# An encoder block on one core: the first stage in a written order, the late expert loads in program order

## The chip, the cores and the metric

One core of a Trainium2 chip runs the whole block in one launch. The metric is the device time of one execution in microseconds (us); lower is better. Two executions differ by about 0.2% without any change.

## What is computed

The reference is one encoder layer on 512 tokens of width 1024, all in float32:

```python
u  = rmsnorm(x, g1)
cb, cc, cx, q, k, v, gc, ga = split(u @ w_in)           # 1024 1024 1024 1024 256 256 1024 1024
yc = (cb * dwconv3(cc * cx)) @ w_conv_out
q  = rope(rmsnorm(q, gq)); k = rope(rmsnorm(k, gk))     # 8 heads of q, 2 of k and v, width 128
ya = attention(q, k, v) @ w_attn_out
x1 = x + (sigmoid(gc) * yc + sigmoid(ga) * ya) @ w_o
out = x1 + moe(rmsnorm(x1, g2))   # 8 groups of 8 experts, best group, best 2 of its experts, width 512
```

## The kernel before

The kernel has two halves. The **mixer** is everything up to `x1`. Its matrices are multiplied in three products: a weight is loaded as float32 (`raw`), cast to a high part (`wh`, ScalarE, L157), and the rest is its low part (`wl`, VectorE, L158); the activations are split in the same way (`uH`, `uL`), and high by high, high by low and low by high are summed in PSUM. `stage` loads and splits one weight slice of 512 KB; `raw`, `wh` and `wl` have two buffers each.

The work is a list of units (`unit`). `run_units` goes through it and stages the weight of the next unit ahead. The framework then orders each engine's instructions by itself: an instruction may run ahead of earlier ones of the same engine when it is ready sooner by the framework's own estimate. `keep_in_program_order` pins one instruction behind what was written before it on its engine.

The units, in order:

- The **first stage**: two halves of v (`v_unit`). Row sums of squares on ScalarE (`norm_stat`), the power -1/2 on POOL, an identity scaled by it (`norm_diag`), and a matmul of x with that identity (`norm_in`, tile `tpu`) which turns and norms a tile of 128 tokens at once; then the gain, the cast and the subtraction, and `o_v`. At its end `rope_tables_in` loads the rope table and the constants.
- The two k heads (`k_unit`), and for each `k_norm_unit`: `norm_rstd` sums squares by matmul (`st_ps`), the power runs on POOL (L262), and a matmul spreads it (`bc`). One cc projection (`fill`) stands between the two.
- For each of 8 heads: q, scores, softmax, turning, values, with the projections cc, cx and cb as fillers.
- The gates gc and ga with `yc`, then `ya`, then `o` (8 slices of `w_o`; the last two are multiplied at the end, bank by bank), and the router's logits.

The **expert half** reads all 64 experts: 192 weight tiles of 2 MB each, in ten rotating slots of the memory that the mixer also uses, and one more tile. `load_weight` issues one on SP's queue. `load_unit` places nine of them into the mixer's list, as its slots come free: 0, 1 and 2 in the gate stages, 3 and 4 behind `ya` units, 5 to 8 behind the `o` units in `LOADS`. `order` gives the slots: 9, 5, 8, 0, 1, 3, 4, 2, 6, 7.

Of the kernel before, what the change touches and what calls it, by code (L numbers as in the profile page):

```python
# [19 lines left out]
P = 128  # L20
T = 512
# [18 lines left out]
def block_kernel(ctx, tc, x, norm1_g, w_in, conv_w, q_norm_g, k_norm_g, w_conv_out,  # L40
                 w_attn_out, w_o, norm2_g, w_group, w_router, w1, w3, w2, rope, out):
    nc = tc.nc
    V, A, G, TE = nc.vector, nc.scalar, nc.gpsimd, nc.tensor
# [34 lines left out]
    def load_x(t):  # L78
        nc.sync.dma_start(xt[:, t, :], x[t * P:(t + 1) * P, :])

    load_x(0)
    load_x(1)
    g1 = cst.tile([P, NK], F32, name="g1")
    A.dma_start(g1, norm1_g[0].rearrange("(k p) -> p k", p=P), allow_slow_non_contiguous=True)
# [6 lines left out]
    warm = cst.tile([P, 1], F32, name="warm")  # L91

# [6 lines left out]
    def load_constants():  # L99
        for nm, src in (("k", k_norm_g), ("q", q_norm_g)):  # L100
            g = src[0].rearrange("(i two) -> two i", two=2)
            for h in range(2):
                for j in range(2):
                    nc.sync.dma_start(gp[nm][h * 64:(h + 1) * 64, j:j + 1], g[(h + j) % 2, :, None],
                                      allow_slow_non_contiguous=True)
        nc.sync.dma_start(cw, conv_w[0].rearrange("w (k p) -> p w k", p=P), allow_slow_non_contiguous=True)
        nc.sync.dma_start(g2, norm2_g[0].rearrange("(k p) -> p k", p=P), allow_slow_non_contiguous=True)
        nc.sync.dma_start(g2j, norm2_g[0].rearrange("(p j) -> p j", j=NK))
        nc.sync.dma_start(wr[:, :, 0:NG], w_group[0].rearrange("(k p) e -> p k e", p=P))
        nc.sync.dma_start(wr[:, :, NG:], w_router[0].rearrange("(k p) e -> p k e", p=P))  # L110
        G.tensor_tensor(wr, wr, g2[:, :, None].to_broadcast([P, NK, NG + NE]), op=OP.mult)
# [16 lines left out]
    with tc.high_priority():  # L128
        make_identity(nc, eye)
        V.tensor_copy(identr, eye)  # L130
    late_x = [lambda: (load_x(2), load_x(3)), lambda: None]

    iog = cst.tile([P, NG], F32, name="iog")
    G.iota(iog, pattern=[[1, NG]], base=-NG, channel_multiplier=0, allow_small_or_imprecise_dtypes=True)
    io32 = cst.tile([P, CAP], F32, name="io32")
    G.iota(io32, pattern=[[1, CAP]], base=0, channel_multiplier=0, allow_small_or_imprecise_dtypes=True)
    iorow = wtile("iorow")[:, :P]
    G.iota(iorow, pattern=[[1, P]], base=0, channel_multiplier=-1, allow_small_or_imprecise_dtypes=True)
    tri = cst.tile([P, P], BF16, name="tri")
    V.tensor_scalar(tri, iorow, 0.0, None, op0=OP.is_gt)  # L140
    onesb = cst.tile([P, 1], BF16, name="onesb")
    V.memset(onesb, 1.0)

    def stage(src, perm=False):
        shape = [P, src.shape[1], src.shape[2]]
        raw = pools["st"].tile(shape, F32, tag="raw", name="raw", bufs=2)
        nc.sync.dma_start(raw, src)
        if late_x:
            late_x.pop()()
# [7 lines left out]
        A.copy(h, r)  # L157
        V.tensor_tensor(l, r, h.bitcast(F32), op=OP.subtract)  # L158
        return wh, wl
# [46 lines left out]
    diags = {}  # L206

    def norm_stat(t):
        c = slice(t, t + 1)
        sq = wtile("sq", "q", 1, [P, D])  # L210
        A.activation(sq, xt[:, t, :], AF.Square, accum_out=ss[:, c])
        V.tensor_scalar(var[:, c], ss[:, c], 1.0 / D, EPS, op0=OP.mult, op1=OP.add)
        G.tensor_tensor(rstd[:, c], var[:, c], nhalf[:, c], op=OP.pow)
# [23 lines left out]
    def rope_tables_in():  # L237
        nc.sync.dma_start(rk[:, 2:4, :], rope.rearrange("a p t -> p a t"))
# [30 lines left out]
    def v_unit(half):  # L269
        def f(wt):  # L270
            if half == 0:
                vacc.extend(pa("o_v") for _ in range(NT))
            for t in range(NT):
                if half == 0:
                    if t + 2 < NT:
                        norm_stat(t + 2)
                    norm_in(t)
                    if t + 2 < NT:
                        norm_diag(t + 2)
                o = vacc[t]  # L280
                c = slice(t * P, (t + 1) * P)
                for k in range(4):
                    kk = 4 * half + k
                    mh, ml = u(kk)
                    mm(o[:, :256], mh[:, c], wt[0][:, k, :], kk == 0, False)
                    mm(o[:, :256], ml[:, c], wt[0][:, k, :], False, False)
                    mm(o[:, :256], mh[:, c], wt[1][:, k, :], False, kk == NK - 1)
                if half == 1:
                    split(vH[:, t * 256:(t + 1) * 256], vL[:, t * 256:(t + 1) * 256], o[:, :256])
            if half == 0:  # L290
                rope_tables_in()
        unit(f, cols(w_in, C_V, 256, 4 * half, 4 * half + 4))
# [3 lines left out]
    def k_unit(g):  # L296
        def f(wt):
            o = pa("o_k")
            proj(o, wt, u)
            kpart[g] = rope_apply(o, rk)  # L300
        unit(f, cols(w_in, C_K + g * HD, perm=True))

    def k_norm_unit(g):
        def f():
            fk, sq = kpart.pop(g)
            r = norm_rstd(sq)
            bc = pt("bc")
            for t in range(NT):
                mm(bc[:, t * P:(t + 1) * P], r[:, 1, t:t + 1].to_broadcast([P, P]), ident, True, True)
            V.tensor_tensor(fk, fk, bc, op=OP.mult)  # L310
            split(kH[:, g * T:(g + 1) * T], kL[:, g * T:(g + 1) * T], fk)
        unit(f)
# [127 lines left out]
    for t in range(2):  # L440
        with tc.high_priority():
            norm_stat(t)
            norm_diag(t)
    v_unit(0)
    v_unit(1)
    k_unit(0)
    k_unit(1)
    k_norm_unit(0)
    fill()
# [98 lines left out]
    def o_unit(kk):  # L548
        def f(wt):
# [9 lines left out]
            elif kk == NK - 1:  # L559
                A.activation(warm, gates["ga"](NK - 1)[:, 0:1], AF.Exp)  # L560
# [56 lines left out]

    load_unit(0)
# [9 lines left out]
    for k in range(NK):  # L628
        ya_unit(k)
        if k in (1, 3):  # L630
            load_unit(3 + k // 2)
# [6 lines left out]
    run_units()  # L638
    mixer.close()
# [267 lines left out]
    pin = tc.keep_in_program_order  # L907

# [41 lines left out]
    def finish_last(X, ws, gt2, c2, y, Sl, wl):  # L950
# [16 lines left out]
        def spread(q):  # L967
# [6 lines left out]
            for h, src in enumerate((o, kept[q])):  # L974
# [6 lines left out]
                (A if h and q == 3 else nc.sync).dma_start(ov[:, 2 * h:2 * h + 2, c0:c1], d)  # L981
# [7 lines left out]
    def store_at(t, n):  # L989
        nc.sync.dma_start(out[t * P:(t + 1) * P, n * 512:(n + 1) * 512], acc_at(t, n))  # L990

    def overflow(tiles):
        n = nc.values_load(ov_tab[0:1, NE:NE + 1], min_val=0, max_val=32)
        with tc.For_i(0, n, 1) as i:
# [12 lines left out]
            for i, w in enumerate((w1, w3, w2)):  # L1007
                src = w[bass.ds(e, 1)].rearrange("o (c p) d -> p (o c) d" if i == 2 else "o (p j) f -> p (o j) f", p=P)
                nc.sync.dma_start(tiles[i], src)
# [103 lines left out]
```

## Time and profile before

| | |
|---|---|
| median of 3 runs | 1471.94 us (1470.76 to 1472.09) |
| the profiled execution | 1478.3 us, span 1476.5 us |
| busy share of the span | TensorE 83%, VectorE 32%, ScalarE 24%, POOL 6% |
| end of the mixer's matmuls | 538.7 us |
| expert weights | 195 loads, 402.7 MB; the rate in the second half is 425 GB/s |

Times in views of the trace are us from the span's start. A line such as `L157` is a line of the kernel; all matmuls have the line of a helper, L74, so they are told apart by tiles. PE is TensorE, DVE VectorE, ACT ScalarE, and SPq the queue of the engine that issues most transfers. A matmul in float32 shows as two records. PEclk is the granted share of TensorE's full clock.

### The profile page before, as it was taken

The page shows a single profiled execution, that of the slowest core. Times are in us where ns is not written, and L with a number is a line of the kernel's source. Part 1 is how long each engine was busy: PE and PEld are TensorE (multiplying, and loading weights), DVE is VectorE, ACT ScalarE, POOL GpSimd, SP SyncE. Part 2 cuts the span into 40 slices and gives each one's busy share as a digit, 9 for nine tenths or more (in the row PEclk, how much of TensorE's full clock was granted, in tenths as well). Part 3 has the DMA queues.
Part 4 walks back from the last instruction along what each step waited for, and adds up shares of the span by engine and source line. Part 5 has one row for each costly group of instructions (what it writes and reads, how often), then busy time and mean ns, then how long its engine had stood idle before and what let it go on. Part 6 is the DMA issues. An engine that isn't in the chain of part 4 may idle for free.

```text
span 1476.5 us, 33402 instructions
## 1 busy us (share of the span) xinstructions
PE 1230.3 (83%) x15172; PEld 911.5 (62%) x15172; DVE 468.9 (32%) x943; ACT 347.6 (24%) x715; POOL 88.0 (6%) x128
## 2 busy tenths in 40 slices
PE   7999999999999988897886685876867758678587
PEld 6788888888887775664654453544545545455454
DVE  4375666623225342332122120220211212212032
ACT  4344444522222232111111111111101111111111
POOL 2200000000002001000000000000000000000000
PEclk9899999999999999999998997998989889888888
DMA  7222222243554749999999999999999999999994
GB/s 218 62 72 71 72 72 71 62 138 87 156 175 128 295 163 427 423 426 425 426 425 426 427 424 427 425 426 425 426 425 427 427 424 427 425 427 425 426 394 156
DMA packets 111664, 449.71 MB, mean 305 GB/s; under 512 B 12577, under 2 KB 85281, under 8 KB 87073
## 3 DMA queue, kind: packets, MB, share of 16 engines
q1 hardware_dynamic: 110208, 447.29, 75.2%
q8 instruction: 120, 1.97, 0.5%
q10 hardware_dynamic: 1312, 0.27, 0.1%
q14 instruction: 24, 0.19, 0.0%
HBM read 445.44 MB, written 2.10 MB: 303 GB/s over the span
## 4 chain that ended last, share of the span: by engine, by line
DMA 49%; PE 47%; issue 2%; DVE 1%; ACT 1%; POOL 0%; SPq 0%; ACTq 0%; DVEq 0%; POOLq 0%
DMA w<-in_w 48%; PE o_g L74 6%; PE h L74 4%; PE o_cc L74 3%; PE o_q L74 3%; PE o_o L74 3%; PE o_cb L74 3%; PE o_cx L74 3%; PE o_yc L74 3%; PE o_ya L74 3%; PE o_c L74 3%; PE y L74 3%; PE o_x L74 2%; PE s L74 2%; PE o_pv L74 1%
## 5 line engine op out<-in xcount | busy, mean ns | idle before, releaser
L74 PE MATMUL h<-w,X 128*32 128x128 f32 x8192 | 290.2, 296 | 109.3 <-DMA w<-in_w 87.8
L74 PEld LDWEIGHTS h<-w,X 128*32 128x32 f32 x8192 | 253.4, 119 | 154.4 <-issue 62.3
L74 PE MATMUL y<-w,gt 128*32 128x256 f32 x2048 | 165.6, 455 | 87.6 <-DMA w<-in_w 61.5
L74 PEld LDWEIGHTS y<-w,gt 128*32 128x32 f32 x2048 | 85.8, 126 | 144.6 <-issue 116.4
L904 ACT COPY Y<-y 32x256 f32<-32x256 f32 x248 | 90.2, 364 | 230.3 <-PE y L74 227.9
L158 DVE TENSOR_TENSOR wl<-raw,wh 128x1024 fp32r<-128x1024 f32 x76 | 99.3, 1309 | 131.6 <-ACT wh L157 130.1
L74 PE MATMUL o_x<-xt,pR 128*32 128x256 f32 x2048 | 133.8, 380 | 6.8 <-issue 4.6
L74 PE MATMUL o_c<-Y,S 128*128 128x512 f32 (+1 forms) x256 | 123.7, 639 | 12.6 <-ACT Y L904 12.6
L157 ACT CAST wh<-raw 128x1024 fp32r<-128x1024 f32 x76 | 80.5, 1060 | 202.7 <-PE o_g L74 67.1
L886 DVE TENSOR_TENSOR sp<-h,sg 128x128 f32<-128x128 f32 x64 | 23.4, 365 | 286.6 <-ACT sg L882 286.6
L847 DVE TENSOR_TENSOR acc<-o_c,acc 128x512 f32<-128x512 f32 x112 | 77.5, 692 | 103.9 <-PE o_c L74 103.9
L74 PEld LDWEIGHTS o_x<-xt,pR 128*32 128x32 f32 x2048 | 81.3, 110 | 40.6 <-issue 8.2
L882 ACT ACTIVATE sg<-h 128x128 f32<-128x128 f32 x64 | 17.8, 278 | 373.6 <-PE h L74 373.6
L732 DVE STREAM_TRANSPOSE X<-xs 128x256 f32<-128x256 f32 x64 | 28.5, 445 | 238.2 <-PE h L74 201.5
L74 PEld LDWEIGHTS o_c<-Y,S 128*128 128x128 f32 (+1 forms) x256 | 50.5, 203 | 82.4 <-issue 50.8
L74 PE MATMUL o_g<-u,wh 128*128 128x512 f32 x256 | 80.5, 395 | 0.0
L870 POOL TENSOR_TENSOR pR<-p,rstd 128x512 f32<-128x512 f32 x15 | 15.6, 1041 | 705.9 <-PE o_x L74 642.1
L74 PEld LDWEIGHTS o_g<-u,wh 128*128 128x128 f32 x256 | 48.2, 188 | 11.2
L74 PE MATMUL o_g<-u,wl 128*128 128x512 f32 x128 | 50.5, 395 | 0.0
L74 PE MATMUL o_o<-wh,m 128*128 128x512 f32 x128 | 41.3, 402 | 1.7 <-ACT wh L157 1.7
L74 PE MATMUL o_cc<-u,wh 128*128 128x512 f32 x128 | 41.5, 406 | 0.0
L74 PE MATMUL o_q<-u,wh 128*128 128x512 f32 x128 | 41.2, 403 | 0.0
(242 smaller groups left out, 1462.0 us busy)
## 6 DMA issues: line engine op xcount, KB each, us to landing
w<-in_w SPq DMA_DIRECT2D x191, 2048.0 KB, 39.6
raw<-in_w_in SPq DMA_DIRECT2D x52, 512.0 KB, 3.8
raw<-in_w_conv_out SPq DMA_DIRECT2D x8, 512.0 KB, 4.1
raw<-in_w_attn_out SPq DMA_DIRECT2D x8, 512.0 KB, 4.2
raw<-in_w_o SPq DMA_DIRECT2D x8, 512.0 KB, 4.4
xt<-in_x SPq DMA_DIRECT2D x4, 512.0 KB, 6.9
w<-in_w SPq DMA_DIRECT2D x4, 512.0 KB, 30.4
out<-acc SPq DMA_DIRECT2D x7, 256.0 KB, 2.4
```

What stands on the lines that cost most here:

```text
L74: return TE.matmul(o, l, r, start=start, stop=stop)
L157: A.copy(h, r)
L158: V.tensor_tensor(l, r, h.bitcast(F32), op=OP.subtract)
L732: V.transpose(X.rearrange("p j s -> p (j s)"), xs.rearrange("p j i -> p (j i)"))
L847: V.tensor_tensor(acc_at(t, n), o, xt[:, t, nsl] if first else acc_at(t, n), op=OP.add)
L870: eng.tensor_tensor(pR, p0.rearrange("p t e s -> p t (e s)"), rstd2[:, :, None].to_broadcast([P, NT, P]), op=OP.mult)
L882: A.activation(sg, h[:, 0:P], AF.Silu)
L886: V.tensor_tensor(sp.rearrange("p (c i) -> p c i", c=4), h[:, P:2 * P].rearrange("p (i c) -> p c i", c=4), sg.rearrange("p (i c) -> p c i" ...
L904: A.copy(d, y[32 * q:32 * q + 32, 0:256])
```

## The change

First, the expert loads and all weight loads from the gate stage on are pinned in program order on SP; the expert loads of the late mixer move to behind `ya` 1 and 4 and `o` 0, 2, 4 and 5. The warming Exp reads a constant instead of a gate.

Second, the first stage is written anew. The gain is loaded as one row and spread over the partitions by two matmuls (`gn`). A tile is scaled by its power and by the gain in one operation (`xs`), turned by plain transposes (`tu`), and cast and subtracted straight from the PSUM bank (`uh`, `ul`), half a tile at a time. `vm` is one of the three products of one half for one token tile. A few matmuls on the identity (`wm`) stand at the start. `V_ORDER` gives the order of all these steps, each pinned on its engine; digits are the token tile, the half, and the product.

Third, the loads of x and of the first weights have an order of their own, and the rope table and constants are loaded, pinned, at the first k unit.

Fourth, `k_norm_unit` is cut in two: both statistics (`k_stat_unit`) come ahead of the cc projection, both spreads behind it.

```diff
-LOADS = (0, 1, 2, 4)
+LOADS = (0, 2, 4, 5)
...
+V_ORDER = (
+    "wm3 gn0 gn1 wm2 ld0 lx1 lx2 lx3 ld1 sq0 rs0 xs00 wh0 xs01 tu00 uh00 wl0 tu01 sq1 vm000 ul00 vm001 "
+    "uh01 rs1 vm002 sq2 ul01 xs10 sq3 xs11 tu10 rs2 tu11 uh10 rs3 xs20 uh11 vm100 ul10 tu20 wh1 vm101 ul11 "
+    "vm102 uh20 wl1 vm010 vm200 vm110 ul20 vm201 xs21 vm011 xs30 vm202 tu21 xs31 tu30 uh21 tu31 uh30 ul21 "
+    "vm012 uh31 ul30 vm300 vs0 vm111 ul31 vm301 vm112 vm302 vs1 vm210 vm310 vm211 vm311 vm212 vm312 vs2 "
+    "vs3 "
+)
...
+                i = call(*args, **kwargs)
+                return tc.keep_in_program_order(i) if pinned else i
+            return issue
...
-    g1 = cst.tile([P, NK], F32, name="g1")
-    A.dma_start(g1, norm1_g[0].rearrange("(k p) -> p k", p=P), allow_slow_non_contiguous=True)
...
+    g1 = slot(3, [1, D], F32, "g1")
+    A.dma_start(g1, norm1_g[0][None, :])
...
+        i = SP.dma_start(raw, src)
+        if nraw[0] < 4 or late:
+            pin(i)
+        nraw[0] += 1
...
-    def norm_diag(t):
-        diags[t] = wtile("diag", "z", 1, [P, 4, P])[:, 0, :]
-        V.tensor_scalar(diags[t], ident, rstd[:, t:t + 1], None, op0=OP.mult)
-
-    def norm_in(t):
-        dg = diags.pop(t)
-        for b in range(2):
-            tp = pt("tpu")
-            tpv = tp.rearrange("p (k c) -> p k c", k=4)
-            for k in range(4):
-                mm(tpv[:, k, :], xt[:, t, (4 * b + k) * P:(4 * b + k + 1) * P], dg, True, True)
-            f = wtile("f")
-            fv = f.rearrange("p (k c) -> p k c", k=4)
-            V.tensor_tensor(fv, tpv, g1[:, 4 * b:4 * b + 4, None].to_broadcast([P, 4, P]), op=OP.mult)
-            h = uH[:, 4 * b:4 * b + 4, t * P:(t + 1) * P]
-            l = uL[:, 4 * b:4 * b + 4, t * P:(t + 1) * P]
-            A.copy(h, fv)
-            (G if b else V).tensor_tensor(l, fv, h.bitcast(F32), op=OP.subtract)
...
+    def gn(b):
+        o = psx("g_b")
+        mm(o, ones[0:1, 0:1].to_broadcast([1, P]), g1[:, b * T:(b + 1) * T], True, True)
+        V.tensor_copy(gb[:, b * T:(b + 1) * T], o)
...
+    def xs(t, b):
+        nsl = slice(b * T, (b + 1) * T)
+        V.scalar_tensor_tensor(xn[:, t, nsl], xt[:, t, nsl], rstd[:, t:t + 1], gb[:, nsl], op0=OP.mult, op1=OP.mult)
+
+    def tu(t, b):
+        tps[t, b] = (psx if t % 2 else pt)("tpu").rearrange("p (k c) -> p k c", k=4)
+        for k in range(4):
+            TE.transpose(tps[t, b][:, k, :], xn[:, t, (4 * b + k) * P:(4 * b + k + 1) * P], ident)
+
+    def u_at(t, b):
+        return (a[:, 4 * b:4 * b + 4, t * P:(t + 1) * P] for a in (uH, uL))
+
+    def uh(t, b):
+        h, _ = u_at(t, b)
+        A.copy(h, tps[t, b])
+
+    def ul(t, b):
+        h, l = u_at(t, b)
+        V.tensor_tensor(l, tps.pop((t, b)), h.bitcast(F32), op=OP.subtract)
+
+    def vm(t, half, part):
+        w, lo = ((0, 0), (1, 0), (0, 1))[part]
+        c = slice(t * P, (t + 1) * P)
+        for k in range(4):
+            kk = 4 * half + k
+            mm(vacc[t][:, :256], u(kk)[lo][:, c], w_v[half][w][:, k, :], kk == 0 and part == 0, kk == NK - 1 and part == 2)
...
+            if g == 0:
+                pinned.append(True)
+                rope_tables_in()
+                pinned.clear()
...
+    def k_stat_unit(g):
+        def f():
+            fk, sq = kpart.pop(g)
+            kpart[g] = fk, norm_rstd(sq)
+        unit(f)
+
     def k_norm_unit(g):
         def f():
-            fk, sq = kpart.pop(g)
-            r = norm_rstd(sq)
+            fk, r = kpart.pop(g)
             bc = pt("bc")
             for t in range(NT):
...
     k_unit(0)
     k_unit(1)
+    k_stat_unit(0)
+    k_stat_unit(1)
+    fill()
     k_norm_unit(0)
-    fill()
     k_norm_unit(1)
...
-                A.activation(warm, gates["ga"](NK - 1)[:, 0:1], AF.Exp)
+                A.activation(warm, nhalf[:, 0:1], AF.Exp)
...
-            nc.sync.dma_start(tile[:, :, c0:c1], src[:, :, c0:c1])
+            ld = SP.dma_start(tile[:, :, c0:c1], src[:, :, c0:c1])
+            if late:
+                pin(ld)
...
+    unit(lambda: late.append(True))
...
-        if k in (1, 3):
-            load_unit(3 + k // 2)
+        if k in (1, 4):
+            load_unit(3 + k // 4)
```

## Rows read from the trace of the kernel before

**Rows 1.** The page, part 2: share of DMA time in 40 equal slices.

```profile
DMA  7222222243554749999999999999999999999994
```

**Rows 2.** Stretches: length, PE busy (matmuls), PEclk, DMA share, GB/s.

```profile
510.00:520.00 10.00, 10.00 (x44) 1.00 0.00 0
538.00:542.00 4.00, 4.00 (x43) 1.00 0.95 369
...
700.00:1400.00 700.00, 512.70 (x9372) 0.88 1.01 426
```

**Rows 3.** Waits of SP's queue: total us, times, longest.

```profile
SPq L612 <- PE o_o L74: 28.8, 1, 28.8
```

**Rows 4.** The chain that ended last, in order: start us, us, what.

```profile
9.75 3.78 PE tpu L74 x16
...
23.73 1.79 PE tpu L74 x16
25.52 6.38 PE o_v L74 x52
...
43.04 0.80 PE st_ps L74 x8
...
44.10 2.00 POOL r L262
...
56.31 1.95 POOL r L262
...
66.15 5.57 PE o_cx L74 x24
...
588.99 7.06 PE o_c L74 x16
```

**Rows 5.** Stretches again, with the granted clock behind the matmul count.

```profile
46.00:48.00 2.00, 1.85 (x9) 0.50 0.72 208
...
60.00:62.00 2.00, 2.00 (x6) 0.50 0.28 84
450.00:452.00 2.00, 0.88 (x4) 1.00 0.00 0
```

**Rows 6.** Timeline of PE at two places late in the mixer.

```profile
449.28 0.40 PE L74 MATMUL o_ya<-OL,wh 128*128 128x512 f32 x1
451.12 0.50 PE L74 MATMUL o_ya<-OH,wl 128*128 128x512 f32 x1 [1.45 <-DVE wl L158]
...
500.85 0.40 PE L74 MATMUL o_o<-wl,m 128*128 128x512 f32 x1
502.95 1.66 PE L74 MATMUL o_o<-wh,m 128*128 128x512 f32 x6 [1.71 <-ACT wh L157]
```

**Rows 7.** Timeline of ACT: behind the second k, and at the router.

```profile
45.19 0.60 ACT L249 ACTIVATE sq<-o_k 128x512 f32<-128x512 f32 x1
...
542.78 0.23 ACT L753 ACTIVATE ex<-ex 128x32 f32<-128x32 f32 x1 [4.00 <-DVE ex L752]
```

**Rows 8.** Timeline of SP's queue: constants, and loads late in the mixer.

```profile
4.41 0.50 SPq L238 DMA_DIRECT2D rk<-in_rope  x1
...
18.00 0.58 SPq L110 DMA_DIRECT2D wr<-in_w_router  x1
...
432.31 0.81 SPq L612 DMA_DIRECT2D w<-in_w  x2
434.61 24.41 SPq L147 DMA_DIRECT2D raw<-in_w_attn_out  x5
...
478.60 0.80 SPq L612 DMA_DIRECT2D w<-in_w  x2
```

**Rows 9.** Tile raw from 425 to 520.

```profile
DMA to landing us min/median/max: 3.5/4.4/13.1
```

**Rows 10.** Groups of DVE up to 80 us, by form.

```profile
L418 DVE SCALAR_TENSOR_TENSOR cc<-mz,cw,cc 128x511 f32<-128x511 f32 x1 | 0.7, 743 | 0.0
```

**Rows 11.** DMA issues up to 40 us.

```profile
g2j<-in_norm_g SPq DMA_DIRECT2D x1, 4.0 KB, 2.6
```

More of the change, by code (lines that the diff above doesn't have):

```diff
@@ L42, in block_kernel, with __init__, __getattr__, issue @@
     nc = tc.nc
-    V, A, G, TE = nc.vector, nc.scalar, nc.gpsimd, nc.tensor
+    pinned = []
+    class Engine:
+        def __init__(self, engine):
+            self.engine = engine
+        def __getattr__(self, name):
+            call = getattr(self.engine, name)
+            def issue(*args, **kwargs):
+                i = call(*args, **kwargs)
+                return tc.keep_in_program_order(i) if pinned else i
+            return issue
+    V, A, G, TE, SP = (Engine(e) for e in (nc.vector, nc.scalar, nc.gpsimd, nc.tensor, nc.sync))
+    pin = tc.keep_in_program_order
     x = x[0]
@@ L127, in block_kernel, with stage @@
     eye = wtile("eye")[:, :P]
[L128 to L144, printed above, removed]
+    make_identity(nc, eye)
+    pinned.append(True)
+    V.tensor_copy(identr, eye)
+    nraw = [0]
+    late = []
+    def stage(src, perm=False, wait=False):
         shape = [P, src.shape[1], src.shape[2]]
         raw = pools["st"].tile(shape, F32, tag="raw", name="raw", bufs=2)
-        nc.sync.dma_start(raw, src)
-        if late_x:
-            late_x.pop()()
+        i = SP.dma_start(raw, src)
+        if nraw[0] < 4 or late:
+            pin(i)
+        nraw[0] += 1
         wh = pools["st"].tile(shape, F32R, tag="wh", name="wh", bufs=2)
@@ L156, in stage @@
             l = l.rearrange("p k (two i) -> p k two i", two=2)
-        A.copy(h, r)
-        V.tensor_tensor(l, r, h.bitcast(F32), op=OP.subtract)
+        parts = [lambda: A.copy(h, r), lambda: V.tensor_tensor(l, r, h.bitcast(F32), op=OP.subtract)]
+        if wait:
+            return (wh, wl), parts
+        for part in parts:
+            part()
         return wh, wl
@@ L267, in block_kernel @@
     vacc = []
[L269 to L292, printed above, removed]
+    vacc.extend(pa("o_v") for _ in range(NT))
@@ new lines, in block_kernel, with ld, wm @@
+    gb = slot(7, [P, D], F32, "gb")
+    xn = slot(8, [P, NT, D], F32, "xn")
+    w_v, w_parts = [], []
+    tps = {}
+    def ld(i):
+        pair, parts = stage(cols(w_in, C_V, 256, 4 * i, 4 * i + 4)[0], wait=True)
+        w_v.append(pair)
+        w_parts.append(parts)
+    def wm(n):
+        for _ in range(n):
+            mm(busy0[:, 0:P], ident, ident, True, True)
+    def gn(b):
+        o = psx("g_b")
+        mm(o, ones[0:1, 0:1].to_broadcast([1, P]), g1[:, b * T:(b + 1) * T], True, True)
+        V.tensor_copy(gb[:, b * T:(b + 1) * T], o)
@@ new lines, in sq, with rs @@
+    def sq(t):
+        junk = wtile("sq", "q", 1, [P, D])
+        A.activation(junk, xt[:, t, :], AF.Square, accum_out=ss[:, t:t + 1])
+    def rs(t):
+        c = slice(t, t + 1)
+        V.tensor_scalar(var[:, c], ss[:, c], 1.0 / D, EPS, op0=OP.mult, op1=OP.add)
+        G.tensor_tensor(rstd[:, c], var[:, c], nhalf[:, c], op=OP.pow)
+    def xs(t, b):
+        nsl = slice(b * T, (b + 1) * T)
+        V.scalar_tensor_tensor(xn[:, t, nsl], xt[:, t, nsl], rstd[:, t:t + 1], gb[:, nsl], op0=OP.mult, op1=OP.mult)
@@ new lines, in vm, with wh, wl, vs @@
+    def vm(t, half, part):
[4 more added lines that the diff above has]
+            mm(vacc[t][:, :256], u(kk)[lo][:, c], w_v[half][w][:, k, :], kk == 0 and part == 0, kk == NK - 1 and part == 2)
+    def wh(i):
+        w_parts[i][0]()
+    def wl(i):
+        w_parts[i][1]()
+    def vs(t):
+        split(vH[:, t * 256:(t + 1) * 256], vL[:, t * 256:(t + 1) * 256], vacc[t][:, :256])
+    busy0 = pt("busy0")
@@ L294, in block_kernel @@
+    steps = dict(ld=ld, lx=load_x, wm=wm, gn=gn, sq=sq, rs=rs, xs=xs, tu=tu, uh=uh, ul=ul, vm=vm, wh=wh, wl=wl, vs=vs)
+    for step in V_ORDER.split():
+        steps[step[:2]](*(int(c) for c in step[2:]))
+    pinned.clear()
     kpart = {}
@@ L297, in f @@
         def f(wt):
+            if g == 0:
+                pinned.append(True)
+                rope_tables_in()
+                pinned.clear()
             o = pa("o_k")
@@ L438, in fill @@
                 fn(k)
[L440 to L445, printed above, removed]
+    iog = cst.tile([P, NG], F32, name="iog")
+    G.iota(iog, pattern=[[1, NG]], base=-NG, channel_multiplier=0, allow_small_or_imprecise_dtypes=True)
+    io32 = cst.tile([P, CAP], F32, name="io32")
+    G.iota(io32, pattern=[[1, CAP]], base=0, channel_multiplier=0, allow_small_or_imprecise_dtypes=True)
+    iorow = wtile("iorow")[:, :P]
+    G.iota(iorow, pattern=[[1, P]], base=0, channel_multiplier=-1, allow_small_or_imprecise_dtypes=True)
+    tri = cst.tile([P, P], BF16, name="tri")
+    V.tensor_scalar(tri, iorow, 0.0, None, op0=OP.is_gt)
+    onesb = cst.tile([P, 1], BF16, name="onesb")
+    V.memset(onesb, 1.0)
     k_unit(0)
     k_unit(1)
+    k_stat_unit(0)
+    k_stat_unit(1)
+    fill()
     k_norm_unit(0)
-    fill()
     k_norm_unit(1)
@@ L638, in block_kernel @@
     run_units()
+    late.clear()
     mixer.close()
@@ L905, in expert @@
         return X
-    pin = tc.keep_in_program_order
     def combine_two(S, Y):
```

30 lines of the change are left out of this document (11 added, 19 removed).

## The prediction

> **What bounds the kernel now.** I read the page's slices first [rows 1]: the DMA engines have two tenths of work in the first third and nine from the sixteenth slice to the end, where they move 425 GB/s. So there are two stages with different limits, TensorE first (83% busy over the span) and DMA then. The chain of waits, grouped, says the same: 48% is DMA into the expert weights, the rest matmuls of the mixer. Then I asked where the two meet. The stretches of time [rows 2] show the transfers idle from 510 to 520, at 369 GB/s by 538 to 542, and at 426 from 554 to 1400. In the idle stretch SP stands 28.8 us in front of one expert load, waiting for the last o_o matmuls [rows 3]: the buffers into which the stream would run are still the mixer's. So nine expert tiles are there when the mixer ends, the stream starts with the mixer's end, and from there the time is bytes over 426 GB/s. A microsecond taken from TensorE ahead of about 538 moves the whole stream, and the end with it. A microsecond behind it is worth nothing.
>
> So the question is how far the mixer's end moves. The chain in order of time [rows 4] shows where TensorE is not streaming. Its first matmul starts at 9.75. It stands at 43.84 and at 56.05 for a POOL power of some 2 us each, and both times it comes back at half clock: the granted clock is 0.50, 1.2 GHz, from 46 to 48 and from 60 to 62 [rows 5]. It stands again late in the mixer, before 451.12 and before 502.95 [rows 6]. Everything between is back to back.
>
> **The change, part by part.**
>
> *The k norms.* Before, the order on TensorE is statistics of k0, wait for POOL, broadcast, cc, statistics of k1, wait, broadcast, q. Now both statistics, then the cc projection, then both broadcasts. From the end of the k projections to the end of q is 43.04 to 66.15 = 23.1 us [rows 4]. The work in it at full clock: two statistics of 0.80, two projections of 5.57 (the length of cx just behind), two broadcasts of 8 records at 1.79 / 16 us each, 0.9 apiece: 14.5 us. The 5.6 us of cc cover the powers: the first is issued within a microsecond of its statistics and takes 2.0; the second must wait for the copies and the square of k1 on ScalarE, 2.9 us after the projection (from the last k1 matmul to the end of its square at 45.79 [rows 7]), then 0.8, then 2.0 again, 5.9 us together against 7.2 us of cc and both statistics. What is late next: nothing by more than a few tenths. If both holes go, 23.1 - 14.5 = 8.6 is won; with the second statistics a little late I take 8.4. The lower bound is one hole only: the second is worth 10.1 - 6.5 = 3.6 (56.05 to 66.15, against one broadcast and one projection).
>
> *The rope table and the constants* move behind the loads of both k weights on SP, with the multiplications that use them pinned on VectorE. Their issue took 4.41 to 18.58 = 14.2 us of SP [rows 8]. The second k weight can be loaded when the second v weight has been split, at about 19; so the constants are out by 33.5, and the raw cc weight behind them lands 3.5 to 4.4 us later [rows 9], at some 37.5, with 2.3 us of split to follow: 39.8. TensorE wants it after both k projections, 30.4 + 11.1 = 41.5. Covered, at nothing, by those projections; without the cover every microsecond counts, and only 1.7 are in hand.
>
> *The first stage.* Gone: the scaled identity, the separate gain multiplication, the POOL subtractions. New: per token tile two scalar_tensor_tensor (0.74 each, by the row of the convolution [rows 10]), 8 transposes, two casts and two subtractions from PSUM (0.62 and 0.68 each, as today's of that size). The matmul work is the same: 64 records of 128 columns at 1.79 / 16 = 7.1, and 96 of o_v at 6.38 / 52 = 11.8, 18.9 us [rows 4]. The start goes by a new chain. The gain row (4 KB, 2.6 us to landing for the nearest transfer [rows 11], issued at about 0.7) is spread over the partitions by two matmuls of 512 columns: eight such matmuls (o_c) took 7.06 us [rows 4], 0.88 each, and twice that at the slow rate with which the first sixteen tpu records ran (3.78 us against 1.79 later). So 3.3 + 3.5 = 6.8; copy 0.69, variance 0.15, power 0.56, scaling 0.74, and hand-overs: first transpose at about 9.2, half a microsecond before today. VectorE then has 3.0 us a tile and serves one tile at a time; in its fixed order the second tile's scaling stands behind the split of the weight and the first tile's subtractions, so TensorE waits some 1.7 us at 12.4. Slow first transposes add 0.6. End: 9.2 + 18.9 + 1.7 + 0.6 = 30.4 against 31.90: 1.5 won. Bounds: at full rate from the start the row spread is 1.8 shorter and nothing is slow, 27.8 (4.1 won); with TensorE at half rate until 22, 34.9 (3.0 lost).
>
> *The expert loads.* The first one, issued at 20.37, goes to the gate stage; slot and data are wanted after 538, so this costs nothing. In the late mixer two loads of 2 MB went out together at 432.31 and two at 478.60 [rows 8], and the raw weights behind them landed up to 13.1 us after their issue, against 3.5 at best [rows 9]. That made the two stalls: 449.28 to 451.12 and 500.85 to 502.95, less 0.23 for the matmul itself [rows 6]: 1.6 + 1.9 = 3.5. Now never two in a row: after ya 1 and 4, after o 0, 2, 4 and 5. The price is that a raw load now stands behind an expert load on SP. The tightest is the third w_o slice: it follows the load that waits for the end of ya (477 with the first stall gone), so it lands about 2 + (2.1 + 0.5 MB) / 0.42 = 8.2 later plus its issue, at 486.4; split by 488.7, wanted at 488.2 to 488.7. I charge 0.3 and take 3.2. All nine tiles are in long before the mixer's end (the last is issued at about 498 for an end at 525), so the stream has the same bytes left.
>
> The Trainium skill (DMA: Bandwidth & Descriptors, Queues, rings and completion order) says that each DMA engine consumes the descriptors of one issuing queue in ring order; if it did not hold, the slice would land at 481 and the 0.3 would fall away. The late landings above agree with it.
>
> *Others.* The warming Exp reads a constant and can run at any time, so the Exp table may have to be loaded again before the softmax of the router; such a load took 1.28 us, and ScalarE is idle for 4.00 just ahead of that Exp [rows 7]: nothing, and 1.28 without that idle time.
>
> **Sum.** 8.4 + 1.5 + 3.2 = 13.1 us. The profiled execution took 1478.3 us with a span of 1476.5, 6.4 above the median of 1471.94; by the sum the next profiled one takes 1465.2, and with the same distance the median becomes **1458.8 us**.
>
> **Rivals.**
> 1. *The clock falls in the first stage.* TensorE now has two holes of some 1.5 and 1.7 us (before the first transpose and before the second tile's) where it had none after 9.75. For it: the waits of 2.00 and 1.95 for POOL at the k norms halved the clock [rows 4, 5]. Against it: idles of 1.45 and 1.71 us late in the mixer [rows 6] left it at 1.00 (the first [rows 5]). Then the stage ends near 34.9, 3.0 later than now: 8.4 - 3.0 + 3.2 = 8.6, **1463.3**. The Trainium skill (TensorE: Matmul & The Clock Gate, Part 1) says that the slow state is the default and that activity releases it, which is this rival; the trace agrees at the k norms and not at the two later idles.
> 2. *Half of the k part stays*, by a statistics matmul that waits for the square on ScalarE, or by the cc weight late behind the constants (1.7 us in hand): 3.6 + 1.5 + 3.2 = 8.3, **1463.6**.
> 3. *The shift does not reach the end.* If the expert stream were limited from its first byte, nothing would move: **1471.9**. Against it: no transfers from 510 to 520 [rows 2], and SP's long wait was for o_o and for no DMA [rows 3].
> 4. *Slower: the expert loads hold up the raw weights.* Six of them now stand ahead of a raw load on a pinned queue. The latest raw load took 13.1 - 3.5 = 9.6 us longer to land than the fastest; its slack is the 13.6 us from its issue to its use less 4.4 of landing and 2.3 of split, 6.9. So up to 2.7 us each, 16.2 in all: 1471.9 - 8.4 - 1.5 + 16.2 = **1478.2**. It turns slower when the six cost more than 9.9 / 6 = 1.65 us on average. Against it: before, two loads ahead of a raw load cost only 1.6.
>
> **How the numbers follow.** All three parts as summed, 1455 to 1463: 0.56, and 0.05 for more than that (the first stage at full rate, 1456.2, and a tail that keeps its clock). Rival 1: 0.16; rival 2: 0.13; rival 3: 0.05; rival 4: 0.05. The first forecast and rivals 1 and 2 all lie in 1452 to 1467, with room for two of them together or for a late cc weight; that leaves about 2 in 10 outside. About 0.2%, 2.9 us, can be told from no change: faster 0.89, same 0.06, slower 0.05.
>
> **What would show it.** The first o_k matmul at about 30.4 (right) or past 32 (rival 1). From the end of o_k to the end of q 15 us, with no POOL wait in the chain and a granted clock of 1.00 there. No stall before ya 3 and o 4. The mixer's last matmul at about 525.6 instead of 538.7, and the DMA stretches after it shifted by the same 13 us at the same 426 GB/s. The prediction is wrong if that shift is under 8 us, or if it is there and the tail takes it back.

## The result, and the profile after

| | before | after |
|---|---|---|
| median of 9 runs each, one chip | 1477.57 us (1470.52 to 1479.74) | 1463.68 us (1457.95 to 1466.49) |
| profiled execution, its span | 1478.3, 1476.5 | 1463.09, 1461.3 |
| mixer's last router matmul ends | 538.72 | 521.42 |

The ratio is 0.9913, 95% interval 0.9895 to 0.9932: 12.8 us won of 1477, between 10.0 and 15.5. Predicted were 13.1 won and 1458.8 us, inside 1452 to 1467. Both kernels' times fall into two groups with some 5 us between them (before: 1470.5 to 1472.1 and 1477.6 to 1479.7; after: 1457.95 and 1458.12, the others from 1462.8 up), so the 0.2% of the opening holds within a group only; what parts them is a finding of the experiments. One execution of the kernel before, in the second session of the experiments, took 2004.35 us and is left out of the ratios.

The predicted signs, in their order. The chain of waits of the kernel after, in order of time (start, us, what); in this trace all lines are L62, a wrapper's, so the tiles tell what is what:

```profile
3.43 3.72 PE g_b L62 x4
...
9.41 1.13 PE tpu L62 x4
...
20.77 1.31 PE tpu L62 x12
22.08 5.78 PE o_v L62 x48
27.86 11.16 PE o_k L62 x48
39.02 0.79 PE st_ps L62 x8
39.80 2.66 PE o_cc L62 x11
42.46 0.79 PE st_ps L62 x8
43.25 3.13 PE o_cc L62 x13
46.38 1.78 PE bc L62 x16
48.16 5.57 PE o_q L62 x24
53.74 5.57 PE o_cx L62 x24
...
420.05 44.63 PE o_ya L62 x192
464.68 42.19 PE o_o L62 x181
```

Against [rows 4]: the first o_k starts at 27.86 and not at 31.90 (30.4 was forecast). From the end of o_k to the end of q it is 14.72 us instead of 23.11, and no POOL stands in it. o_ya and o_o run as unbroken pieces; the breaks of [rows 6] are gone. The clock, in stretches (length; busy time and count of PE, PEld, DVE, ACT, POOL; granted clock; DMA share; GB/s), against [rows 5] and [rows 2]:

```profile
42.00:46.00 4.00, 4.00 (x23) 3.39 (x23) 1.26 (x3) 0.00 (x0) 2.71 (x3) 1.00 0.48 135
46.00:50.00 4.00, 4.00 (x27) 3.61 (x26) 2.65 (x4) 2.42 (x4) 0.00 (x0) 1.00 0.06 10
...
520.00:530.00 10.00, 8.74 (x128) 7.30 (x130) 7.46 (x47) 4.44 (x10) 1.34 (x3) 1.00 0.95 377
700.00:1400.00 700.00, 507.62 (x9217) 352.37 (x9213) 140.12 (x318) 105.23 (x292) 25.09 (x50) 0.89 1.01 425
```

The clock is full where it was half, and the stream is there from 520 on and not from 538, at 425 GB/s. SP's queue, against [rows 8], and the landing of the raw weights from 405 to 510, against [rows 9]:

```profile
434.82 0.57 SPq L62 DMA_DIRECT2D w<-in_w  x1
440.07 4.79 SPq L62 DMA_DIRECT2D raw<-in_w_attn_out  x2
...
468.26 0.43 SPq L62 DMA_DIRECT2D w<-in_w  x1
```

```profile
DMA to landing us min/median/max: 3.5/4.4/8.9
```

No two expert loads in a row, and the latest raw load takes 8.9 us and not 13.1. So each predicted step is there, and the mixer ends 17.3 us earlier, where 13.1 was forecast. The span is shorter by 15.2. Three questions follow: where do the 4.2 us more at the mixer's end come from, where do 2.1 of them go, and why does the ratio say 12.8?

### The profile page after: what moved, and what is told of

Same layout as the page of the kernel before. It is cut to its first block, busy times and chain, and to the rows that moved or that the text cites. A ratio compares the mean times of both kernels' runs of the same rounds, so it can differ in the third digit from the quotient of the medians.

```text
span 1461.3 us, 33363 instructions
## 1 busy us (share of the span) xinstructions
PE 1221.9 (84%) x15154; PEld 912.0 (62%) x15154; DVE 472.5 (32%) x945; ACT 346.4 (24%) x715; POOL 80.8 (6%) x124
## 4 chain that ended last, share of the span: by engine, by line
PE 52%; DMA 44%; issue 2%; DVE 1%; ACT 1%; POOL 0%; SPq 0%; POOLq 0%; ACTq 0%
DMA w<-in_w 44%; PE o_g L62 6%; PE h L62 5%; PE o_c L62 5%; PE y L62 4%; PE o_cc L62 3%; PE o_q L62 3%; PE o_cb L62 3%; PE o_cx L62 3%; PE o_ya L62 3%; PE o_yc L62 3%; PE o_o L62 3%; PE o_x L62 3%; PE s L62 2%; PE o_pv L62 2%
## 5 line engine op out<-in xcount | busy, mean ns | idle before, releaser
L62 PE MATMUL h<-w,X 128*32 128x128 f32 x8192 | 293.3, 299 | 117.8 <-DMA w<-in_w 95.5
L62 PEld LDWEIGHTS h<-w,X 128*32 128x32 f32 x8192 | 255.3, 120 | 163.7 <-issue 77.3
L62 PE MATMUL y<-w,gt 128*32 128x256 f32 x2048 | 159.3, 443 | 87.1 <-DMA w<-in_w 67.2
L62 PEld LDWEIGHTS y<-w,gt 128*32 128x32 f32 x2048 | 87.5, 124 | 139.0 <-issue 112.9
L62 ACT COPY Y<-y 32x256 f32<-32x256 f32 x248 | 90.2, 364 | 223.3 <-PE y L62 220.9
L62 DVE TENSOR_TENSOR wl<-raw,wh 128x1024 fp32r<-128x1024 f32 x76 | 100.7, 1325 | 131.0 <-ACT wh L62 129.6
L62 PE MATMUL o_x<-xt,pR 128*32 128x256 f32 x2048 | 136.0, 386 | 5.5 <-issue 3.1
L62 PE MATMUL o_c<-Y,S 128*128 128x512 f32 (+1 forms) x256 | 118.8, 618 | 12.6 <-ACT Y L62 12.6
L62 ACT CAST wh<-raw 128x1024 fp32r<-128x1024 f32 x76 | 80.6, 1060 | 199.7 <-PE o_g L62 67.1
L62 DVE TENSOR_TENSOR acc<-o_c,acc 128x512 f32<-128x512 f32 x124 | 85.7, 691 | 107.5 <-PE o_c L62 107.4
L62 DVE TENSOR_TENSOR sp<-h,sg 128x128 f32<-128x128 f32 x64 | 23.2, 362 | 284.6 <-ACT sg L62 284.6
L62 DVE STREAM_TRANSPOSE X<-xs 128x256 f32<-128x256 f32 x64 | 28.5, 445 | 251.3 <-PE h L62 214.0
L62 ACT ACTIVATE sg<-h 128x128 f32<-128x128 f32 x64 | 17.8, 278 | 385.8 <-PE h L62 385.8
L62 PEld LDWEIGHTS o_x<-xt,pR 128*32 128x32 f32 x2048 | 83.8, 111 | 38.5 <-issue 7.3
L62 PEld LDWEIGHTS o_c<-Y,S 128*128 128x128 f32 (+1 forms) x256 | 48.6, 195 | 78.3 <-issue 47.7
L62 PE MATMUL o_g<-u,wh 128*128 128x512 f32 x256 | 80.4, 395 | 0.0
L62 PEld LDWEIGHTS o_g<-u,wh 128*128 128x128 f32 x256 | 48.2, 188 | 11.1
L62 POOL TENSOR_TENSOR pR<-p,rstd 128x512 f32<-128x512 f32 x15 | 15.6, 1039 | 706.3 <-PE o_x L62 641.6
L62 PE MATMUL o_g<-u,wl 128*128 128x512 f32 x128 | 50.5, 395 | 0.0
L62 PE MATMUL o_o<-wh,m 128*128 128x512 f32 x128 | 40.7, 399 | 0.0
L62 PE MATMUL o_q<-u,wh 128*128 128x512 f32 x128 | 40.3, 396 | 0.0
L62 PE MATMUL o_cc<-u,wh 128*128 128x512 f32 x128 | 40.2, 395 | 0.0
```

Of the source, the lines that this page charges most:

```text
L62: i = call(*args, **kwargs)
```

## The experiments

Unless said otherwise a time is the median of all runs of that kernel, and a ratio is to the kernel before on the same chip (its medians there: 1473.18, 1476.62 and 1474.71 in the three sessions). All traces put together, in us ("k part": end of the k projections to the end of q; "combine": the 16 matmuls that add the outputs of the experts 60 and 61 to the sum, behind expert 61; they are the last of this kind, and a shorter tail for the last two experts follows):

| kernel | time, ratio [interval] | first o_k | k part | mixer's end | span less that | combine |
|---|---|---|---|---|---|---|
| before | | 31.90 | 23.11 | 538.72 | 937.8 | 11.86 |
| after | 1463.68, 0.9913 [0.9895, 0.9932] | 27.86 | 14.72 | 521.42 | 939.9 | 11.80 |
| e1 | 1471.04, 0.9974 [0.9957, 0.9992] | 27.95 | 21.66 | 528.44 | 941.5 | 11.74 |
| e2 | 1464.44, 0.9944 [0.9923, 0.9965] | 27.97 | 14.70 | 526.45 | 936.4 | 7.13 |
| e3 | 1468.0, 0.9955 [0.9938, 0.9973] | 30.95 | 14.71 | 524.49 | 935.1 | 7.13 |
| e4 | 1458.06, 0.9908 [0.9884, 0.9932] | 26.17 | 14.71 | 519.86 | 934.9 | 7.13 |
| e5 | 1464.93, 0.9910 [0.9883, 0.9937] | 27.97 | 14.72 | 521.50 | 942.4 | 14.02 |
| e6 | 1474.38, 1.0005 [0.9984, 1.0026] | 31.51 | 18.72 | 533.94 | 937.4 | 11.71 |
| e7 | 1468.65, 0.9952 [0.9933, 0.9971] | 32.07 | 14.72 | 530.67 | 933.5 | 7.13 |
| e8 | 1456.96, 0.9882 [0.9852, 0.9911] | 26.15 | 14.72 | 519.69 | 935.6 | 7.13 |
| e9 | 1462.75, 0.9918 [0.9898, 0.9938] | 27.86 | 14.71 | 521.42 | 940.6 | 7.13 |
| e10 | 1473.69, 0.9993 [0.9976, 1.0009] | 31.65 | 20.24 | 535.78 | 935.4 | 7.13 |
| e11 | 1459.34, 0.9902 [0.9877, 0.9927] | 26.19 | 14.71 | 519.72 | 937.5 | 7.13 |
| e12 | 1462.68 (one run) | 27.96 | 14.72 | 524.35 | 936.6 | 7.13 |

### The first stage: e3 and e4

e3 is the kernel after with the turns of the rows as matmuls with the identity:

```diff
-            TE.transpose(tps[t, b][:, k, :], xn[:, t, (4 * b + k) * P:(4 * b + k + 1) * P], ident)
+            mm(tps[t, b][:, k, :], xn[:, t, (4 * b + k) * P:(4 * b + k + 1) * P], ident, True, True)
```

> The changed kernel with each of the 32 plain transposes made a float32 matmul with the identity, all else in place. Theory: a transpose shows one record of 0.11 us and a matmul two, so the first stage has 32 records or 3.5 us more of TensorE work, its end goes from 27.9 to about 31, and the time up by 3 to 3.5 us, to about 1466.5. Rival, that the first stage is bound by VectorE's chain and not by TensorE: its end moves by less than 1 us.

Its chain:

```profile
15.26 2.05 PE tpu L62 x16
...
22.52 2.68 PE tpu L62 x24
25.20 5.75 PE o_v L62 x48
30.95 9.05 PE o_k L62 x39
```

24 records where the kernel after has 12. The tile has 64 records against 32, the stage ends at 30.95 against 27.86, and the mixer ends 3.07 later. A plain transpose of a float32 tile is one record, a matmul of the same shape is two, at the same 0.11 us each. And 30.95 is within 0.6 of the 30.4 that the prediction summed with 64 records: the rest of its first-stage sum is right as a sum, though not term by term (below). The median of 1468.0 us is 4.3 above the kernel after, in another session.

e4 puts the first tile's scaling ahead of the spread of the gain row's second half, and leaves out two of the five matmuls on the identity at the start (`wm2`):

```diff
-    "wm3 gn0 gn1 wm2 ld0 lx1 lx2 lx3 ld1 sq0 rs0 xs00 wh0 xs01 tu00 ...
+    "wm3 gn0 ld0 lx1 lx2 lx3 ld1 sq0 rs0 xs00 gn1 wh0 xs01 tu00 ...
```

> The changed kernel with the second half of the gain spread only after the first scaling, and without the two last identity matmuls ahead of the first transpose. Theory: today the variance of tile 0 waits on VectorE behind the copy of the second half of the gain row until 7.78; without that the first transpose starts at about 7.7 instead of 9.41, the first stage ends 1 to 1.7 us earlier and so does the kernel, about 1462. Rival, that the slow rate of the first matmuls only starts its count later: the first transpose is early, but the stage ends at the same 27.9.

In its chain the first o_k stands at

```profile
26.17 11.14 PE o_k L62 x48
```

So the stage ends 1.69 earlier, and the mixer 1.56 earlier. The first transpose starts at 7.71 instead of 9.41; which share `wm2` has in that was not tested by itself. In time the two medians, 1458.06 and 1463.68, are from different sessions, and the intervals of the ratios overlap, so the gain is shown in the trace alone.

### The k norms: e1 and e7

e1 is the kernel after with the old order, e7 the kernel before with the new one. The diff of e1:

```diff
     k_unit(1)
     k_stat_unit(0)
+    k_norm_unit(0)
+    fill()
     k_stat_unit(1)
-    fill()
-    k_norm_unit(0)
     k_norm_unit(1)
```

> The changed kernel with the k norms in the old order (statistics, broadcast, cc, statistics, broadcast). Theory of three separate parts: the two waits for POOL and the half clock behind them come back, from the end of the k projections to the end of q it takes about 23 us instead of 14.7, and the time is 8.4 us above the changed kernel, some 1471. Rival, that the waits went because the first stage and the constants moved: the stretch stays near 15 us and the time near that of the changed kernel, 1463.

> The kernel before with nothing but the new order of the k norms. Theory: from the end of the k projections to the end of q it takes 14.7 us instead of 23.1, no half clock, and the mixer's end and the time go down by 8.4: about 1464 to 1465 against 1473. Rival, that it needs the constants' new place too: a new wait for a raw weight or for the statistics keeps half of it, 1468 or more.

e7 gives exactly the 8.4 us in its trace (23.11 to 14.72):

```profile
43.23 0.79 PE st_ps L74 x8
...
57.95 5.57 PE o_cx L74 x24
```

Its median of 1468.65 is above the 1464 to 1465 that was expected, but so was the kernel before in that session (1476.62 and not 1473); 8.0 us lie between them. e1 gives only 6.9 in its trace. The reason lies in rows of e1 and e6 (e6, below, has the old order and differs from the kernel before in its tail alone). The chain of e1 and one of its stretches:

```profile
40.15 2.02 POOL r L62
42.17 0.04 issue
42.21 1.95 PE bc L62 x8
```

```profile
42.00:46.00 4.00, 3.79 (x14) 3.36 (x15) 1.72 (x3) 0.62 (x1) 1.39 (x2) 0.57 0.49 135
```

The chain of e6 at the same place, and a stretch there:

```profile
43.71 2.00 POOL r L262
45.76 1.16 PE bc L74 x8
46.92 5.12 PE o_cc L74 x22
```

```profile
46.00:48.00 2.00, 2.00 (x14) 1.78 (x14) 1.04 (x2) 0.32 (x1) 0.94 (x1) 1.00 0.85 252
```

The same wait of 2.0 us for the same power. In e1 the broadcast behind it runs at half clock and takes 1.95 us, in e6 it keeps the full clock and takes 1.16; in e10 the clock stayed behind the first wait and fell behind the second. So the old order's k part is 23.1, 21.7, 20.2 or 18.7 us from one execution to the next, and the new one's is 14.70 to 14.72 in all ten traces that have it. The two waits themselves cost 4.0 (18.72 less 14.72); the clock behind them cost between 0 and 4.4 in these four traces. The prediction read its 8.4 from an execution in which it fell both times.

### The expert loads: e2 and e12

e2 puts the loads back at their old places and takes SP's fixed order away; e12 takes only the fixed order away.

```diff
-LOADS = (0, 2, 4, 5)
+LOADS = (0, 1, 2, 4)
...
-    unit(lambda: late.append(True))
...
-        if k in (1, 4):
-            load_unit(3 + k // 4)
+        if k in (1, 3):
+            load_unit(3 + k // 2)
```

> The changed kernel with the expert loads at their old places and without pins on SP. Theory: two loads of 2 MB go out in a row again, TensorE waits for the fourth ya and the fifth o weight, 1.6 and 1.9 us, and the mixer's end comes 3.5 to 5 us later: about 1467. Rival, that pins alone and not the loads' places won the time, or that the router's end of the mixer got shorter for another reason: the two waits come back but the end of the mixer moves by less than 2 us.

> The kernel after with the four expert loads of each late stage at their new places, but SP left to order the raw w_o and expert loads itself. If the places are what won the 3.6 us in the late mixer (no two expert loads in a row ahead of a raw load): no stall before ya 3 and o 4, last raw landing under 10 us, the mixer's last matmul at 521 to 522 as in the kernel after. If the program order on SP is what won them: two loads go out together again, the raw weights land up to 13 us after issue, and the mixer ends at 525 to 527.

TensorE's timeline in e2 has the stalls again, and the raw weights (410 to 515) land late:

```profile
438.76 0.50 PE L62 MATMUL o_ya<-OH,wl 128*128 128x512 f32 x1 [1.35 <-DVE wl L62]
...
490.65 1.67 PE L62 MATMUL o_o<-wh,m 128*128 128x512 f32 x6 [1.71 <-ACT wh L62]
```

```profile
DMA to landing us min/median/max: 3.4/4.6/13.2
```

The mixer ends 5.0 later. In time this is not as plain: the median of 1464.44 missed the expected 1467 and is only 0.8 above the kernel after, from another session; by the ratios, 0.9944 against 0.9913, e2 is 4.6 slower, but their intervals overlap. So the 5.0 are shown in the trace. SP's queue in e12, with the new places and no fixed order:

```profile
419.95 0.82 SPq L62 DMA_DIRECT2D w<-in_w  x2
422.29 24.40 SPq L62 DMA_DIRECT2D raw<-in_w_attn_out  x5
...
466.29 0.80 SPq L62 DMA_DIRECT2D w<-in_w  x2
```

Left to itself, SP's order has the loads two by two again, the stall before the fourth ya slice is back (1.26 us, 1.35 in e2), the one in o is not, and the mixer ends 2.9 later than with the fixed order, just below the 525 to 527 expected for that case. So of the 5.0 us some 2.1 come with the places alone, and the 2.9 need the order as well.

### The two groups of times: e5, e6, e8, then e9, e10, e11

TensorE's timeline of the kernel after, near the end:

```profile
1406.05 1.96 PE L62 MATMUL h<-w,X 128*32 128x128 f32 x64 [0.40 <-DMA w<-in_w]
1411.06 1.93 PE L62 MATMUL y<-w,gt 128*32 128x256 f32 x32 [3.05 <-DMA w<-in_w]
1413.84 11.80 PE L62 MATMUL o_c<-Y,S 64*128 64x512 f32 x16 [0.85 <-ACT Y L62]
```

The combine behind expert 61 takes 11.80 us, for most of it at half clock, 1.2 GHz (0.60 granted over the whole). In e12 nearly the same three waits stand before it (0.29, 3.04 and 0.85), and it takes 7.13 at full clock:

```profile
1413.47 1.93 PE L62 MATMUL y<-w,gt 128*32 128x256 f32 x32 [3.04 <-DMA w<-in_w]
1416.25 7.13 PE L62 MATMUL o_c<-Y,S 64*128 64x512 f32 x16 [0.85 <-ACT Y L62]
```

I first took the place to be the experts 57 to 59 and gave TensorE 72 idle matmuls there, in the kernel after (e5), the kernel before (e6) and e4 (e8). e9, e10 and e11 are the same three kernels with 20 idle matmuls in each of the experts 60 and 61 instead; the diff is that of e9. The first call of `hold` stands behind each half of h, the second behind y.

```diff
+    def hold(n):
+
+        if held:
+            for _ in range(n):
+                tc.keep_in_program_order(mm(held[0][:, 0:P], ident, xt[:, 0, 0:P], True, True))
...
+            hold(12 if o0 else 4)
...
+        hold(4)
...
+        if e in (60, 61):
+            held[:] = [pt("held")]
```

> The changed kernel with 72 matmuls on the identity (8 behind each half of h and behind y, for experts 57 to 59), which compute nothing that is used: TensorE has less idle time there while it waits for weights. Theory: the times of the changed kernel fall into 1458 and 1463 to 1466 because TensorE's clock sometimes falls to half just ahead of the last full combine (o_c 11.8 us instead of 7.1); with the clock held all runs lie near 1457 to 1459. Rival, that the two groups of times come from the memory: the spread stays, and the added matmuls cost up to some us.

> The kernel before with the same matmuls for experts 57 to 59. With the clock held in both, the distance to the run of the changed kernel with it is the change alone: by the theory that every microsecond of the mixer reaches the end, 17.3 us (the mixer's last matmul moved from 538.7 to 521.4), so about 1474 to 1475 for it if the other is 1457. Rival, that some of the shift is lost in the expert stream: 13 us or less, about 1470 to 1471.

> The changed kernel with the scaling of the first half tile ahead of the spread of the second half of the gain, and the clock held for experts 57 to 59: first stage 1.7 us shorter, no high group of times. Theory: 1455.5 to 1456.5 in all runs, the fastest of all. Rival, that the held clock costs something: no faster than 1458.

> The kernel after, with 20 idle matmuls of 128 columns in each of the experts 60 and 61 (four behind the first half of h, twelve behind the second, four behind y), so that TensorE's two waits for expert 61's weights (0.40 and 3.05 us in the profile after) and the one before the last full combine (0.85) shrink. Theory (those waits are what brings the clock down at that combine, and the two groups of times come from it): the combine's 16 matmuls take 7.1 us and not 11.8, the granted clock of the stretch is 1.00, and all runs lie in the low group, 1457 to 1460. Rival (the fall has another cause): the combine still takes 11.8 us in some runs, and both groups remain, 1458 and 1463 to 1466.

> The kernel before with the same 20 idle matmuls in each of the experts 60 and 61, its mixer in the order it had. Theory: the group at 1477 to 1480 goes and all runs lie at 1470 to 1474; the distance to the kernel after with the same matmuls is then that of the change alone, 12 to 17 us (the mixer's end moved by 17.3 and the starts of the combines by 15 to 17). Rival (the clock at the last combine is not what parts the groups): both groups remain.

> The first token tile's scaling put ahead of the spread of the second half of the gain row (1.7 us off the first stage, measured) together with the idle matmuls in the experts 60 and 61. Theory: 1.7 below the kernel after with the same idle matmuls, at 1455 to 1458 in all runs. Rival: the 1.7 us are lost in the expert stream, whose combines moved by 15 to 17 us for a mixer that ended 17.3 earlier: the same time as without.

e5 refuted the place: the waits in front of the combine were still there (1.09 and 3.04 where the kernel after has 0.40 and 3.05), the combine took 14.02, and two groups remained (1458.9 and 1459.6, and four from 1464.4 to 1465.8). e6 changed nothing in time and shows above all the k part without a clock fall. e8 had four of five runs at 1456.7 to 1457.1 and one at 1464.17; its combine kept the clock, but nothing held it there. In e8 and e4 the clock fell one step sooner instead: behind the same wait of 3.04 and 3.05 the 32 matmuls of y took 3.31 and 3.25 us (granted clock 0.59 and 0.58), where the kernel after has 1.93, and the clock was back when the combine began.

With the idle matmuls in 60 and 61 the combine takes 7.13 in all three traces; e9's, with the combine behind expert 59 ahead of it:

```profile
1385.40 9.17 PE L62 MATMUL o_c<-Y,S 128*128 128x512 f32 x16 [0.83 <-ACT Y L62]
...
1417.10 1.93 PE L62 MATMUL y<-w,gt 128*32 128x256 f32 x32
1418.96 1.16 PE L62 MATMUL held<-xt,identr 128*128 128x128 f32 x8
1420.05 7.13 PE L62 MATMUL o_c<-Y,S 64*128 64x512 f32 x16
```

The range of the runs shrinks: before from 12.4 us (1469.65 to 1482.07, 17 runs) to 5.1 (1471.62 to 1476.75, 12 runs), after from 8.5 to 4.0 (1459.87 to 1463.82, 6 runs), e11 to 1.45 (4 runs). The upper group is gone, but so is the lower one, and the forecasts missed, 1457 to 1460 for e9, 1470 to 1474 for all runs of e10, 1455 to 1458 for e11: TensorE comes to the combine at 1420.05 in e9 and not at 1413.84, without a wait since 1394. Not all of these 6.2 us are the cover's: in this execution the clock fell at the combine behind expert 59, which takes 9.17 us and 7.13 in the kernel after. In e11, where it did not fall there, the combine starts 2.0 later than in e4 (1415.16 and 1413.15). So the cover costs some 2 to 4 us in these two executions, and in these runs about what it saves: e9's median is 0.9 below that of the kernel after, and e11 at 1459.34 is no faster than e4. The idle matmuls are pinned, too, and change the order of the matmuls around them (o_x no longer runs between those of h); that was not tested apart from the cover.

The column "span less that" in the table says the same of all traces. Without idle matmuls in 60 and 61 it is 933.5 to 936.6 where the combine kept the clock (six traces) and 937.4 to 942.4 where it did not (five): 4.4 us between the means. The place is shown by the stretch from this combine's start to the start of the last matmuls: 38.9 to 40.9 us in the five traces with the combine at half clock, 32.8 to 36.1 in the nine others. So this clock costs the end some 4 to 5 us, most of the 6.5 us between the means of the two groups of the kernel after, and it is the best account of them; of that kernel itself there is one trace, from the upper group, so that the lower one has the full clock there is not shown directly. The kernel before has a second such fall, in its k part, which may be why e10 still spreads over 5.1.

The pair e9 and e10 was to give the change alone, with 12 to 17 us. It gave 10.9 in medians. In the profiled pair e10's k part is 20.24 and not 23.11, and its mixer ends 14.4 us behind e9's; e9 had the clock fall behind expert 59.

## Why the prediction was right, and where its terms were off

| term at the mixer's end | predicted | in the profiled pair | what the runs say |
|---|---|---|---|
| k norms | 8.4 (3.6 to 8.6) | 8.4 | 4.0 to 8.4 from one execution to the next |
| first stage | 1.5 (-3.0 to 4.1) | 4.0 | 3.1 of it are the transposes (e3) |
| expert loads | 3.2 | 4.9 | 5.0 by e2 |
| constants moved | 0 | 0 | raw cc weight lands at 34.5 (37.5 forecast), wanted at 39.8 |
| sum | 13.1 | 17.3 | 12.5 to 17.3 against three traces with the old k order |

*First stage.* The mis-sized term is "the matmul work is the same, 64 records". It is 32, 3.5 us instead of 7. The Trainium skill (TensorE: Matmul & The Clock Gate, Part 4) says that a transpose is a matmul with a mode switched on and the identity as one operand, some 275 ns in one kernel (the tile that it names is bf16). The median record of tpu has 273 ns here, of a float32 tile, but with the matmul of e3 it has 275, so a record's length does not tell the two apart. That the transpose is one record, and the matmul two, only the trace showed. The slow start was as forecast (g_b 3.72 us for the spread, 9.41 against 9.2 for the first transpose). The predicted hole of 1.7 us before the second tile measured 0.33 in TensorE's timeline:

```profile
11.20 1.23 PE L62 MATMUL o_v<-wh,u 128*128 128x256 f32 x4
12.22 1.05 PE L62 MATMUL o_v<-wl,u 128*128 128x256 f32 x4
13.08 0.71 PE L62 MATMUL o_v<-wh,u 128*128 128x256 f32 x4
14.11 1.32 PE L62 MATMUL tpu<-identr,xn 128*128 128x128 f32 x8 [0.33 <-DVE xn L62]
```

The first o_v matmuls ran slow and filled it: eight take 1.88 us from start to start, where at full rate they take 0.96 (8 x 5.78 / 48). So the hole was priced too high and the slow work too low. From the first transpose to the first o_k it is 18.45 us; 32 records at 1.31 / 12 and 96 at 5.78 / 48 are 15.1; of the 3.4 more only 0.5 are waits (0.33, and 0.15 before the third tile), where 1.7 of waits and 0.6 of slow work had been forecast. The sum of the corrections: 1.5 + 3.1 for the transposes - 0.55 for the rest (30.95 against 30.4 in e3) = 4.05. That 27.86 is the lower bound of the prediction (27.8, everything at full rate) is luck: the start was slow, and the transposes were short.

*k norms.* Mechanism and cover right: both powers lie behind o_cc, and the sum of 14.5 measured 14.72. The order is not quite the one that was forecast: 11 of the 24 records of o_cc run ahead of the second statistics, and the 3.13 us behind them cover the second power. The size is right for the execution that it was read from, and larger than the other three traces with the old order give (4.0 to 6.9). The medians of e7 and e1, 8.0 and 7.4 us away from their neighbours, don't settle which is usual.

*Expert loads.* The two stalls went, as priced: o_ya is 1.71 shorter (46.34 to 44.63), o_o's stall 1.87. The 0.3 charged for the third w_o slice did not come; no raw load was late. What the prediction did not have are 1.3 us at the end of the mixer: from o_o's start to the last router matmul it was 59.91 and is 56.74. 0.7 of them are waits there for xT and xt (idle in the last stretch 1.14 before, 0.42 after); e2 has the old waits again (1.15), so they go with the loads. The rest I did not trace.

*From the mixer's end to the end of the span.* "Shifted by the same 13 us" was too simple. Over the 14 traces a straight line through the start of the combine behind expert 59 against the mixer's end has a slope of 0.89, with a scatter of 0.8 us: by it 17.3 become 15.4. In the profiled pair this start moved by 15.4 (1401.23 to 1385.80) and the span by 15.2; both had the combine behind expert 61 at half clock. Why the slope is not 1 stays open; the stream runs at 425 to 426 GB/s in both. With 12.5 to 17.3 at the mixer's end the line gives 11.2 to 15.4, around the 12.8 of the ratio. The ratio also mixes the groups: the lower ones of the two kernels are 13.3 us apart in their means and the upper ones 14.1, but 7 of 9 runs of the kernel after are in the upper one, and 5 of 9 of the kernel before. So the 13.1 came out right by errors that cancel, and that is luck: 4.2 too little at the mixer's end in the pair, less what the other executions, the slope and the share of the groups take off. "A microsecond behind [the mixer's end] is worth nothing" does not hold for the tail either: the clock at one combine there is worth 4 to 5 us. And the half of the chain that is not DMA is not all mixer; the h, y, o_c and o_x of the page's chain are expert matmuls, 12% of the span.

*Rivals.* The measured 1463.68 is, to 0.4 us, the number of rivals 1 and 2 (1463.3 and 1463.6); that they did not happen is seen in the traces and not in the time. 1, the clock in the first stage: the slow rate was there at the start, with a granted clock that reads 1.00 from 2 us on, so what made it stays open; the stage ended at 27.86 and not at 34.9. 2, half of the k part stays: no, no wait is left and the clock is 1.00. 3, the shift doesn't reach the end: no, in e1, e3 and e7 the medians moved with the mixer's end (e2's moved less). 4, the expert loads hold up the raw weights: no, and the old order did so (e2).

That the absolute time came out 4.9 above 1458.8 is mostly the yardstick: the three runs of before had a median of 1471.94, the nine beside the result 1477.57.

## What to carry to other kernels

Where a wait sometimes halves TensorE's clock, price the wait and the clock behind it as two terms, and read the second from more than one execution: here one trace said 8.4 us, and four said 4.0 to 8.4. Turn float32 rows with a transpose and not with a matmul; the scale that rode on that matmul found room here in a VectorE operation that was needed anyway (0.75 us a half tile with it, 0.68 without). And where transfers share one queue, spreading them in the program can be half the work; without a fixed order the queue had them two by two again.

## What was not expected of the hardware

- A float32 transpose of 128x128 runs as one record, a float32 matmul of that shape as two (32 and 64 records, 3.1 us of the stage in e3).
- Identical code with identical waits meets either clock: behind a wait of 2.0 us at the k norms the broadcast took 1.16, 1.37 or 1.95 to 2.08 us, and behind waits of 3.04 or 3.05 and 0.85 the combine behind expert 61 took 7.13 or 11.8. Idles of 1.45 and 1.71 late in the mixer [rows 6] left 1.00. The Trainium skill (TensorE: Matmul & The Clock Gate, Part 1) says that the gate's observation runs freely and isn't started by the kernel; these pairs agree with it, and no run here tests it.
- This clock alone is worth 4.7 us in that combine and up to 4.4 in the old k part. Together that is 9.1 of the 12.4 us over which the runs of the kernel before spread; that those runs differ by these two places was not shown run by run.
